# VectorE and ScalarE in written order, and two transposes moved off TensorE, in a hybrid attention and RWKV layer

## The chip, the cores and the metric

The kernel runs on one core of a Trainium2 chip, in one launch. The metric is the device time of one execution in microseconds (us). The core's engines work side by side, each through its own queue in order: TensorE (PE: matmuls, and transposes as matmuls with an identity), VectorE (DVE), ScalarE (ACT), GpSimd (POOL) and SyncE (SP), which here issues nearly all DMAs. Where one engine needs another's result it waits on a semaphore, and all that stands behind it in its queue waits too.

## The reference

One layer over 256 tokens of width 4096, all float32. One projection of the input feeds forgetting attention (FoX: 16 heads of 128), RWKV-7 time mixing (32 heads of 64) and a gate; the gated heads go through an output projection, and a layer norm follows:

```python
proj = einsum('bsd,dc->bsc', x, w_in)      # [fox q|k|v|f, rwkv r|k|v|w|a, gate z]
fox  = softmax(q k^T / sqrt(128) + sum of log f, causal) v
rw   = rw + (rw_prev - rw) * mu_shift      # token shift of the rwkv columns
# per frame: S = S diag(decay) + (S a) b^T + v k^T ;  y = S r
rwkv = groupnorm(y) * gn_gain + gn_bias + bonus
h    = concat(fox, rwkv) * silu(z)
x    = layernorm(ALPHA * x + h @ w_out)
```

The decay and the rate a come from two low-rank ("lora") projections.

## The kernel before

**Main stream.** The weights are read once, in tiles of 128x1024 float32 (two contraction steps of 512 columns). SP loads each by DMA (L220, name w, or wo for the output weights). Each is split into two parts for TensorE's fast float format: ScalarE casts the high half (L141, w_..h) and VectorE subtracts it from the original (L142, w_..l). The input is split the same way, and a product is three matmuls (L147 to L149 in `mm`: high by high, low by high, high by low); a tile is 12 matmuls of 128x512. The input projection runs over 8 pairs n (two groups of 128 channels each) and 4 blocks b of 16 tiles each: b = 0 makes the rwkv r and k, b = 1 the values, b = 2 and 3 the attention's q and k and the gates of one group each. The very first block comes from smaller pieces, together with the lora columns. Then the output projection runs over 8 column blocks of 16 tiles each (`project`, L880 to L882); blocks 0 and 1 are interleaved up to their last tiles, because the last h come late. `weights` keeps three tiles ready: the split of a tile is issued when the matmuls of the tile two before it are.

**Side work.** After every six matmuls `slot()` moves each generator in `sides` on by one `yield`, so a tile has two slots. `wait(W[...])` lets so many slots pass; W holds these numbers. The generators are: `ahead` (`lora`, then `prepare(i)` for each group: decay, its running sum and exponentials, key norms, the matrices BK and lt), `chain` (`forget` for the forget gates, then `rwkv(n)`), `unload` (moves a block's columns from PSUM out, turns them in 32x32 blocks by VectorE, through DRAM and back, and starts `fox(i)`) and `fox` (one attention head).

`rwkv(n)` works on a pair: the 64x64 and 32x32 triangles (gp), a substitution of 31 steps on VectorE (L600 a product, L603 a sum, one step a slot), the values less their mean (L623, SV; ScalarE copies them to UV at L626), further triangles (qt, xp, Q, X), then four chunks in turn (rh, R, up, UV, sp, SV), the readout yp, its norm, and the gated h with its two halves (`gate`, L380 to L384). BK has to be turned for the chunk updates (its turned copy is BKt): in the kernel before by 8 PE transposes a pair (L571) into PSUM and two ScalarE copies of 128x512 (L572). In `fox` the probabilities (lg) are turned the same way, by three PE transposes (L758) and one ScalarE copy of 128x384 (L760) to pT, which the last product (fop, L765) reads.

**Order.** The order of instructions on an engine is set by a scheduler when the program is built. `tc.keep_in_program_order(...)` makes an instruction keep the place in which it was written; `tc.issue_after(...)`, in `behind`, lets some come after the latest split. Before, only SP's DMAs and a few VectorE and ScalarE instructions were held so; the rest was moved by the scheduler.

**Output projection.** `load_tok(b)` loads the residual's columns and the norm's gain and bias, splits the latter (rr, rh, rt, rows: L866 to L872; each one buffer), `add` adds the residual and takes the statistics (L891, L892), `gain` multiplies by the norm's gain (L896) and for the first four blocks splits the result (gh at L899, gl at L900).

Of the kernel before, what the change touches and what calls it, by code (L numbers as in the profile page):

```python
# [17 lines left out]
P = 128  # L18
S = 256
# [26 lines left out]
W = {"fo": 3, "vs": 2, "np": 4, "gp": 5, "tp": 4, "d1": 8, "d2": 12, "xp": 3, "fs": 4, "fp": 5}  # L46
# [38 lines left out]
def layer(ctx: ExitStack, tc: tile.TileContext, xt, xtok, w_main, w_lora, w_first, muv, w_o, up, par, mulora, fbias, lng, lnb, cst, out):  # L85
    nc = tc.nc
    PS = bass.MemoryType.PSUM
# [36 lines left out]
    nc.vector.memset(warm, 0.0)  # L124
    tc.keep_in_program_order(nc.scalar.activation(warm, warm, AF.Tanh))
# [10 lines left out]
    latest = [None]  # L136

    def split(src, n, name, pool=wpool, tag="", cols=1024):
        hi = pool.tile([P, cols], F32R, tag="wh" + tag, name=name + "h", bufs=4 if pool is wpool else 1)
        lo = pool.tile([P, cols], F32R, tag="wl" + tag, name=name + "l")  # L140
        nc.scalar.copy(hi[:, :n], src[:, :n])  # L141
        latest[0] = nc.vector.tensor_tensor(lo[:, :n], src[:, :n], hi[:, :n].bitcast(F32), ALU.subtract)  # L142
        return hi, lo
# [14 lines left out]
    for n, (k0, k1) in enumerate(pieces):  # L158
        for k in range(k0, k1):
            t = xpool.tile([P, 2, S], F32R, tag=f"x{k}", name=f"x{k}")  # L160
            r = x_raw[n][:, (k - k0) * S : (k - k0 + 1) * S]
            tc.keep_in_program_order(nc.scalar.copy(t[:, 0, :], r))
            nc.vector.tensor_tensor(t[:, 1, :], r, t[:, 0, :].bitcast(F32), ALU.subtract)
            xs.append(t)
# [9 lines left out]
    nc.vector.tensor_scalar(half, prm[:, 0:2, :], 0.5, None, ALU.mult)  # L174
    nkk = const.tile([P, G], F32, name="nkk")
    nc.vector.tensor_scalar(nkk, prm[:, PAR.index("k_k"), :], -1.0, None, ALU.mult)
    omm = const.tile([P, 3, G], F32, name="omm")
    nc.vector.tensor_scalar(omm, prm[:, 7:10, :], -1.0, 1.0, ALU.mult, ALU.add)
    oml = const.tile([LORA, 2], F32, name="oml")
    nc.vector.tensor_scalar(oml, mul, -1.0, 1.0, ALU.mult, ALU.add)  # L180
    ika = PAR.index("k_a")
    hka = const.tile([P, 2, G], F32, name="hka")
    nc.vector.tensor_scalar(hka[:, 0, :], prm[:, ika, :], 0.5, None, ALU.mult)
    nc.vector.tensor_scalar(hka[:, 1, :], prm[:, ika, :], -0.5, 1.0, ALU.mult, ALU.add)
    gneps = const.tile([P, 1], F32, name="gneps")
# [37 lines left out]
    def fetch():  # L223
        while len(raws) < 3 and stream:
            load()
        if raws:
# [49 lines left out]
    def lerp(p, mu, om, dst):  # L276
        nc.scalar.mul(dst, p, om)
        nc.vector.scalar_tensor_tensor(dst[:, 1:], p[:, : S - 1], mu, dst[:, 1:], ALU.mult, ALU.add)
# [3 lines left out]
    def issue(out, src):  # L282
        tc.keep_in_program_order(nc.sync.dma_start(out=out, in_=src))
# [19 lines left out]
    for m in range(2):  # L303
        nc.scalar.copy(lw[:, m, :], acc_l[m][:, :LW])
        nc.scalar.copy(bk_0[:, m, :P], acc_l[m][:, LW:LA])
    ff = []

    def lora():
# [9 lines left out]
        nc.vector.tensor_scalar(u, fft[:NF, :S], fb, None, ALU.add)  # L318
        ff.append(u)
        for j in range(2):  # L320
            t = rp.tile([LORA, S], F32, tag="zt", name=f"lw{j}")
            lerp(lt2[:LORA, j * S : (j + 1) * S], mul[:, j : j + 1], oml[:, j : j + 1], t)
            if j == 0:
                nc.scalar.activation(t, t, AF.Tanh)
            nc.scalar.copy(lr[:, j, 0, :], t)
            nc.vector.tensor_tensor(lr[:, j, 1, :], t, lr[:, j, 0, :].bitcast(F32), ALU.subtract)
# [4 lines left out]
    def forget():  # L331
# [5 lines left out]
        nc.vector.tensor_scalar(e, u, -1.0, None, ALU.mult)  # L337
        nc.vector.tensor_tensor(e, e, u, ALU.min)
        nc.scalar.activation(e, e, AF.Exp)
        e1 = ft("fe1")  # L340
        nc.vector.tensor_scalar(e1, e, 1.0, None, ALU.add)
        lg = ft("flg")
        nc.scalar.activation(lg, e1, AF.Ln)
        rest = ft("frest")
        nc.vector.tensor_scalar(rest, e1, -1.0, None, ALU.add)
        nc.vector.tensor_tensor(rest, e, rest, ALU.subtract)
        nc.vector.reciprocal(e1, e1)
        nc.vector.tensor_tensor(rest, rest, e1, ALU.mult)
        nc.vector.tensor_tensor(lg, lg, rest, ALU.add)
        nc.vector.tensor_scalar(u, u, 0.0, None, ALU.min)  # L350
        nc.vector.tensor_tensor(lg, u, lg, ALU.subtract)
        nc.vector.memset(e, 1.0)
        nc.vector.tensor_tensor_scan(rest, e, lg, 0.0, ALU.mult, ALU.add)
        nc.vector.tensor_scalar(lg, rest, -1.0, None, ALU.mult)
# [5 lines left out]
        nc.vector.tensor_copy(ct, ctp[:, : 2 * NF])  # L360
# [8 lines left out]
    def silu2(z, key):  # L369
        th = t256("zt", key + "t")  # L370
        nc.scalar.activation(th, z, AF.Tanh, scale=0.5)
        nc.vector.scalar_tensor_tensor(z, th, 1.0, z, ALU.add, ALU.mult)
        szs[key] = z

    def gate(y, key, k):
# [4 lines left out]
        nc.vector.scalar_tensor_tensor(h, y, 0.5, szs[key], ALU.mult, ALU.mult)  # L380
        pool, tag, bufs = (rp, "hl", 2) if far else (xpool, f"x{k}", 1)
        hl = pool.tile([P, 2, S], F32R, tag=tag, name=f"hl{k}", bufs=bufs)
        nc.scalar.copy(hl[:, 0, :], h)
        nc.vector.tensor_tensor(hl[:, 1, :], h, hl[:, 0, :].bitcast(F32), ALU.subtract)  # L384
# [34 lines left out]
    def front(i):  # L419
        upt = ups[i]  # L420
        uph = rp.tile([LORA, 2, P], F32R, tag="uph", name=f"uph{i}")
        nc.scalar.copy(flat(uph), flat(upt))
        upl = rp.tile([LORA, 2, P], F32R, tag="upl", name=f"upl{i}")
        nc.vector.tensor_tensor(flat(upl), flat(upt), flat(uph).bitcast(F32), ALU.subtract)
# [9 lines left out]
        nc.scalar.activation(tw, lp[:, :S], AF.Tanh, scale=0.5, bias=half[:, 0, i : i + 1])  # L434
        ta = rt(f"ta{i}")
        nc.scalar.activation(ta, lp[:, S:], AF.Tanh, scale=0.5, bias=half[:, 1, i : i + 1])
        yield
        nc.vector.tensor_scalar(tw, tw, -0.5 * DECAY, -0.5 * DECAY, ALU.mult, ALU.add)
        L = rt(f"L{i}")
        nc.vector.tensor_tensor_scan(L, cs[:, C_SCAN : C_SCAN + S], tw, 0.0, ALU.mult, ALU.add)  # L440
        eL = rp.tile([P, NCH, C + 1], F32, tag="eL", name=f"eL{i}")
        nc.gpsimd.memset(eL[:, :, 0:1], 1.0)
        nc.scalar.activation(eL[:, :, 1:], ch(L), AF.Exp)
        eI = t256("eI", f"eI{i}")
        nc.scalar.activation(eI, L, AF.Exp, scale=-1.0)
        yield
        am = t256("am", f"am{i}")
        nc.scalar.activation(am, ta, AF.Identity, scale=hka[:, 0, i : i + 1], bias=hka[:, 1, i : i + 1])
        ae = t256("ae", f"ae{i}")
        nc.vector.scalar_tensor_tensor(ae, ta, 1.0, eI, ALU.add, ALU.mult)  # L450
# [4 lines left out]
    def gather_heads(src, name):  # L455
        t = rp.tile([P, 2 * S], F32, tag="shl", name=f"hq{name}")
        nc.vector.transpose(t, src)
        r = rp.tile([P, 2, QS], F32, tag="hr", name=f"hr{name}", bufs=2)
        nc.vector.tensor_reduce(r[:, 0, :], t.rearrange("p (q f) -> p q f", f=B), AX.X, ALU.add)
# [5 lines left out]
    def spread(dst, val):  # L465
        nc.vector.transpose(dst.rearrange("p (q f) -> p q f", f=B), val.unsqueeze(2).to_broadcast([P, val.shape[1], B]))
# [4 lines left out]
    def prepare(i):  # L471
# [16 lines left out]
        nc.vector.tensor_tensor(k, kr, am, ALU.mult)  # L488
        sb = rp.tile([P, 2, S], F32, tag="Nb", name=f"sb{i}")
        nc.scalar.activation(sb[:, 0, :], kr, AF.Square, scale=column("k_k", i))  # L490
        nc.vector.scalar_tensor_tensor(sb[:, 1, :], r, column("r_k", i), k, ALU.mult, ALU.mult)
# [5 lines left out]
        nc.scalar.copy(q["lc"][:, u, :], eL[:, :, C])  # L497
        nc.vector.scalar_tensor_tensor(lt[0][:, :, 0, :], ch(kr), nkk[:, i : i + 1], eL[:, :, 0:C], ALU.mult, ALU.mult)
        nc.vector.tensor_tensor(lt[0][:, :, 1, :], ch(r), eL[:, :, 1:], ALU.mult)
        nc.scalar.copy(lt[1][HALF[1]], lt[0][HALF[1]])  # L500
        yield
        for j in range(2):
            h = HALF[j]
            nc.vector.tensor_tensor(BK[h, :, KB[j][1]], ch(k)[h], ch(eI)[h], ALU.mult)
        yield from wait(W["np"] if n else 2 * W["np"])
        nc.vector.tensor_tensor(hr[:, 0, :], hr[:, 0, :], hr[:, 1, :], ALU.add)
        n2 = hr[:, 1, : QS // 2]
        nc.vector.tensor_scalar(n2, hr[:, 0, : QS // 2], 1e-24, None, ALU.max)
        nc.vector.reciprocal(n2, n2)
# [5 lines left out]
        nc.vector.scalar_tensor_tensor(ae, ae, 0.5, in2, ALU.mult, ALU.mult)  # L515
        for j in range(2):
            h = HALF[j]
            nc.vector.scalar_tensor_tensor(BK[h, :, KB[j][0]], ch(kr)[h], column("k_k", i)[h], ch(ae)[h], ALU.mult, ALU.mult)
# [3 lines left out]
    def rwkv(n):  # L522
# [27 lines left out]
        for u in range(2):  # L550
            for j in range(2):
                h = HALF[j]
                nc.vector.tensor_tensor(gb[j][h, u], gv[u][j][h], m(h), ALU.mult)
# [3 lines left out]
            nc.sync.dma_start(out=flat(nb[:, u]), in_=nd[u].rearrange("q c r s -> (q c) (r s)").unsqueeze(1).to_broadcast([16, NG, B * B]))  # L557
        for u in range(2):
            for j in range(2):
                o = HALF[1 - j]  # L560
                nc.vector.tensor_tensor(lt[j][o, u], gv[u][j][o].rearrange("p c (x t) -> p c x t", x=2), m(o).rearrange("p c (x t) -> p c x t", x=2), ALU.mult)
# [5 lines left out]
        BKt = rp.tile([P, 2, NCH, P], F32, tag="shl", name=f"BKt{n}")  # L567
        for u in range(2):
            tp = pst(f"tp{n}_{u}")
            for c in range(NCH):  # L570
                nc.tensor.transpose(tp[:, c * P : (c + 1) * P], BK[:, u, c, :], ident)  # L571
            nc.scalar.copy(flat(BKt[:, u]), tp)  # L572
        yield from wait(W["d1"])

        def turns():
            yield from wait(4)
            vst = UVt.rearrange("p u c j v -> p u (c j v)")[:, 0].rearrange("p (m q) -> p m q", m=2)
            for a in range(2):
                tc.keep_in_program_order(nc.vector.transpose(vst[:, a, :], vs_[n][:, a, :]))
# [6 lines left out]
            nc.vector.tensor_tensor(flat(bon), flat(bon), flat(vv[n]), ALU.mult)  # L586
            for u in range(2):
                nc.scalar.activation(bon[:, u], bon[:, u], AF.Identity, bias=column("gn_bias", i0 + u))
# [6 lines left out]
        for u in range(2):  # L595
            nc.scalar.copy(prod[:, u], ev)
            nc.scalar.copy(xc[:, u, :, B - 1 : B], ev[:, :, B - 1 : B])
# [520 lines left out]
```

## Time and profile before

| what | us |
|---|---|
| three runs | 1940.58, 1937.24, 1934.83 (median 1937.24) |
| profiled execution | 1935.4, span 1933.6 |
| tile of the main stream, split to split | 2.72 |
| mean granted TensorE clock | 0.999 of full speed |

In rows of groups, "| 31.0, 704 | 6.6 <-ACT bk" reads: busy 31.0 us in all, 704 ns for one, and 6.6 us of idle time of the engine just before them, most of it ended by that releaser. In the timeline a row is start, duration, engine, line, operation, output and inputs, and in brackets the idle time before it and what ended it. In the list of waits the three numbers are total, times and longest.

### The profile page before, as it was taken

To read this page: it belongs to the slowest core of one execution; us is meant where nothing else is said; L and a number is where in the kernel's file an instruction comes from. 1 tells how busy PE (TensorE), PEld (TensorE's weight loads), DVE (VectorE), ACT (ScalarE), POOL (GpSimd) and SP (SyncE) were. 2 spreads that over 40 slices of the span, in tenths; PEclk is the share of its full clock that TensorE was granted. 3 is DMA by queue.
4 is the path that set the end of the run, shared out by engine and by line. 5 is a ranking of instruction groups with operands and counts; after the bars stand their busy time and mean duration, and the time that the engine had idled before them with its cause. 6 is when DMAs were issued, how large, how long until landed. Compare 5 with 4: busy or idle time off the path is not lost.

```text
span 1933.6 us, 27829 instructions
## 1 busy us (share of the span) xinstructions
PE 1916.5 (99%) x9897; PEld 1594.4 (82%) x9897; DVE 1363.2 (71%) x2323; ACT 963.5 (50%) x1447; POOL 124.2 (6%) x207
## 2 busy tenths in 40 slices
PE   9999999999999999999999999999999999999998
PEld 9888788788888888888888888888888888888886
DVE  6677768857786778677857795779577856755555
ACT  6554464455545644464456444645464554443332
POOL 0020002000200020002000200020001001000000
PEclk9999999999999999999999999999999999999999
DMA  9577667767686778677867677777777777766564
GB/s 343 152 237 229 200 199 215 223 201 216 206 238 198 214 214 236 195 216 211 233 195 220 211 228 202 217 212 220 215 210 221 238 278 242 251 199 197 186 204 166
DMA packets 269391, 420.04 MB, mean 217 GB/s; under 512 B 142338, under 2 KB 169364, under 8 KB 269252
## 3 DMA queue, kind: packets, MB, share of 16 engines
q1 hardware_dynamic: 268820, 417.58, 70.7%
q8 instruction: 77, 1.26, 0.3%
q10 hardware_dynamic: 432, 0.69, 0.1%
q14 instruction: 62, 0.51, 0.1%
HBM read 388.55 MB, written 29.64 MB: 216 GB/s over the span
## 4 chain that ended last, share of the span: by engine, by line
PE 95%; DVE 3%; DMA 1%; issue 0%; ACT 0%; SPq 0%; DVEq 0%; ACTq 0%
PE acc L147 23%; PE acc L149 23%; PE acc L148 23%; PE oacc L880 6%; PE oacc L881 6%; PE oacc L882 6%; PE gp L536 1%; PE rh L647 1%; PE up L678 1%; PE sp L687 1%; PE accl L149 0%; PE accl L148 0%; PE accl L147 0%; PE yp L709 0%; DVE prod L600 0%; DVE xc L603 0%
## 5 line engine op out<-in xcount | busy, mean ns | idle before, releaser
L603 DVE TENSOR_REDUCE xc<-prod 128x8 f32<-128x16 f32 (+30 forms) x248 | 73.1, 295 | 6.5
L600 DVE TENSOR_TENSOR prod<-Nb,xc 128x8 f32<-128x8 f32 (+30 forms) x248 | 71.4, 288 | 6.5 <-DMA Nb<-nd 0.4
L142 DVE TENSOR_TENSOR w_6l<-w,w_6h 128x1024 fp32r<-128x1024 f32 x31 | 37.9, 1222 | 37.5 <-ACT w_6h L141 25.4
L142 DVE TENSOR_TENSOR w_5l<-w,w_5h 128x1024 fp32r<-128x1024 f32 x31 | 41.3, 1333 | 29.5 <-PE acc L149 23.2
L142 DVE TENSOR_TENSOR w_12l<-w,w_12h 128x1024 fp32r<-128x1024 f32 x31 | 38.0, 1227 | 33.5 <-issue 13.8
L740 POOL TENSOR_SCALAR_AFFINE_SELECT nb<-nb 128x128 f32<-128x128 f32 x32 | 15.8, 498 | 705.2 <-DMA nb<-ncd 514.0
L141 ACT CAST w_12h<-w 128x1024 fp32r<-128x1024 f32 x31 | 32.5, 1050 | 48.4 <-DMA w<-in_w_main_dram 19.1
L142 DVE TENSOR_TENSOR w_10l<-w,w_10h 128x1024 fp32r<-128x1024 f32 x31 | 37.9, 1223 | 24.0 <-issue 17.9
L142 DVE TENSOR_TENSOR w_7l<-w,w_7h 128x1024 fp32r<-128x1024 f32 x31 | 37.9, 1222 | 22.1 <-PE acc L149 15.3
L141 ACT CAST w_13h<-w 128x1024 fp32r<-128x1024 f32 x31 | 32.5, 1049 | 40.7 <-PE acc L148 29.0
L141 ACT CAST w_5h<-w 128x1024 fp32r<-128x1024 f32 x31 | 32.6, 1051 | 40.1 <-PE acc L148 37.1
L142 DVE TENSOR_TENSOR w_11l<-w,w_11h 128x1024 fp32r<-128x1024 f32 x31 | 37.9, 1221 | 19.7 <-PE acc L149 19.7
L142 DVE TENSOR_TENSOR w_8l<-w,w_8h 128x1024 fp32r<-128x1024 f32 x31 | 37.8, 1219 | 19.7 <-PE acc L149 15.4
L149 PE MATMUL acc<-w_7l,x 128*128 128x512 f32 x124 | 47.7, 394 | 3.9 <-DVE w_7l L142 3.8
L147 PE MATMUL acc<-w_8h,x 128*128 128x512 f32 x124 | 50.8, 410 | 0.0
L147 PE MATMUL acc<-w_7h,x 128*128 128x512 f32 x124 | 49.9, 403 | 0.2 <-ACT w_7h L141 0.2
L142 DVE TENSOR_TENSOR w_13l<-w,w_13h 128x1024 fp32r<-128x1024 f32 x31 | 37.9, 1222 | 17.2 <-issue 8.3
L147 PE MATMUL acc<-w_3h,x 128*128 128x512 f32 x124 | 49.9, 403 | 0.0
L147 PE MATMUL acc<-w_5h,x 128*128 128x512 f32 x124 | 49.8, 402 | 0.0
L147 PE MATMUL acc<-w_11h,x 128*128 128x512 f32 x124 | 49.8, 402 | 0.0
L147 PE MATMUL acc<-w_15h,x 128*128 128x512 f32 x124 | 49.6, 400 | 0.0
L147 PE MATMUL acc<-w_9h,x 128*128 128x512 f32 x124 | 49.2, 397 | 0.0
(813 smaller groups left out, 6518.7 us busy)
## 6 DMA issues: line engine op xcount, KB each, us to landing
w<-in_w_main_dram SPq DMA_DIRECT2D x496, 512.0 KB, 3.9
wo<-in_w_o_dram SPq DMA_DIRECT2D x128, 512.0 KB, 4.4
bt<-bk SPq DMA_DIRECT2D x88, 128.0 KB, 4.2
Nb<-nd SPq DMA_DIRECT2D x16, 512.0 KB, 4.7
hd<-hl SPq DMA_DIRECT2D x29, 256.0 KB, 3.5
h<-hd SPq DMA_DIRECT2D x29, 256.0 KB, 6.5
wr<-in_w_first_dram SPq DMA_DIRECT2D x15, 384.0 KB, 6.4
lr<-in_w_lora_dram SPq DMA_DIRECT2D x14, 336.0 KB, 5.2
```

The source lines that it names most:

```text
L141: nc.scalar.copy(hi[:, :n], src[:, :n])
L142: latest[0] = nc.vector.tensor_tensor(lo[:, :n], src[:, :n], hi[:, :n].bitcast(F32), ALU.subtract)
L147: nc.tensor.matmul(acc[:, :n], xs[k][:, 0, tt], hi[:, o : o + n], start=(k == 0), stop=False)
L148: nc.tensor.matmul(acc[:, :n], xs[k][:, 1, tt], hi[:, o : o + n], start=False, stop=False)
L149: nc.tensor.matmul(acc[:, :n], xs[k][:, 0, tt], lo[:, o : o + n], start=False, stop=(k == KT - 1))
L536: nc.tensor.matmul(o, BK[h, u, c, :], lt[j][h, u, c], start=True, stop=True)
L600: first = nc.vector.tensor_tensor(prod[:, :, :, s + 1 :], nb[:, :, s : s + 1, s + 1 :].to_broadcast([P, 2, NJ, w]), xc[:, :, :, s + 1 :], ...
L603: nc.vector.tensor_reduce(xc[:, :, :, s : s + 1], prod[:, :, :, s:], AX.X, ALU.add)
L647: nc.tensor.matmul(rh[:, u * P : (u + 1) * P], LT[:, u, c, 0:P], flat(SVt[:, u, c]), start=True, stop=True)
L880: nc.tensor.matmul(acc, ht[k][:, 0, tt], hi, start=(k == 0), stop=False)
L881: nc.tensor.matmul(acc, ht[k][:, 1, tt], hi, start=False, stop=False)
L882: nc.tensor.matmul(acc, ht[k][:, 0, tt], lo, start=False, stop=(k == KT - 1))
```

## The change

`pin` is `tc.keep_in_program_order`, and it is put around nearly every VectorE and ScalarE instruction (splits, casts, side work, output projection); `latest` and `behind` go. Further `yield`s cut side work into smaller lots: in `rwkv` after the DMAs of each u, after the second masks of each u, in the copies of BKt, between the two halves of SV (with the later wait two shorter), after the square root; in `fox` between the exponentials and the reciprocals (the wait fp one shorter); after each `shifted`; between the two `silu2`. W["fo"] goes from 3 to 7. BK's and the probabilities' PE transposes are replaced: VectorE turns 32x32 blocks in place, and copies put the blocks where they belong, 16 of 32 rows a pair for BKt, all by GpSimd and for three of the four chunks, and 16 of 32x96 a head for pT, half by ScalarE and half by GpSimd.

In numbers, over the whole program: TensorE 112 transposes fewer (64 + 48); VectorE 32 transposes more (128x384 each); ScalarE 32 evictions fewer and 128 copies more; GpSimd 256 copies more; SP the same number of DMAs.

```diff
-W = {"fo": 3, "vs": 2, ...
+W = {"fo": 7, "vs": 2, ...
+    pin = tc.keep_in_program_order
...
-        nc.scalar.copy(hi[:, :n], src[:, :n])
-        latest[0] = nc.vector.tensor_tensor(lo[:, :n], src[:, :n], hi[:, :n].bitcast(F32), ALU.subtract)
+        pin(nc.scalar.copy(hi[:, :n], src[:, :n]))
+        pin(nc.vector.tensor_tensor(lo[:, :n], src[:, :n], hi[:, :n].bitcast(F32), ALU.subtract))
...
-        BKt = rp.tile([P, 2, NCH, P], F32, tag="shl", name=f"BKt{n}")
+        BKt = rp.tile([P, 2, NCH - 1, P], F32, tag="shl", name=f"BKt{n}")
         for u in range(2):
-            tp = pst(f"tp{n}_{u}")
-            for c in range(NCH):
-                nc.tensor.transpose(tp[:, c * P : (c + 1) * P], BK[:, u, c, :], ident)
-            nc.scalar.copy(flat(BKt[:, u]), tp)
+            v = flat(BK[:, u, : NCH - 1, :])
+            pin(nc.vector.transpose(v, v))
+        for a in range(4):
+            for b in range(4):
+                nc.gpsimd.tensor_copy(BKt[B * b : B * (b + 1), :, :, B * a : B * (a + 1)], BK[B * a : B * (a + 1), :, : NCH - 1, B * b : B * (b + 1)])
+            if a % 2:
+                yield
...
-            tc.keep_in_program_order(nc.scalar.copy(UV[j][o], SV[j][o]))
+            pin(nc.scalar.copy(UV[j][o], SV[j][o]))
             nc.gpsimd.memset(SV[j][HALF[j], :, 0, :], 0.0)
-        yield from wait(W["d2"] - 1)
+            yield
+        yield from wait(W["d2"] - 3)
...
-        yield from wait(W["fp"])
-        pt = pst(f"fpt{i}")
-        for m in range(3):
-            nc.tensor.transpose(pt[:, m * P : (m + 1) * P], lg[:, m, :], ident)
-        pT = rp.tile([P, 3 * P], F32, tag="nb", name=f"pT{i}")
-        nc.scalar.copy(pT, pt[:, : 3 * P])
+        yield from wait(W["fp"] - 1)
+        pin(nc.vector.transpose(flat(lg), flat(lg)))
+        pT = rp.tile([P, 3, P], F32, tag="nb", name=f"pT{i}")
+        for a in range(4):
+            for b in range(4):
+                pin((nc.gpsimd.tensor_copy if b % 2 else nc.scalar.copy)(pT[B * b : B * (b + 1), :, B * a : B * (a + 1)], lg[B * a : B * (a + 1), :, B * b : B * (b + 1)]))
+        pT = flat(pT)
         yield from wait(W["fo"])
...
-        nc.vector.tensor_scalar(rt_, rh.bitcast(F32), cs[0:6, C_ROW : C_ROW + 1], None, ALU.mult)
-        nc.vector.scalar_tensor_tensor(rows[0:6, o], rr, cs[0:6, C_ROW + 1 : C_ROW + 2], rt_, ALU.mult, ALU.add)
+        pin(nc.vector.tensor_scalar(rt_, rh.bitcast(F32), cs[0:6, C_ROW : C_ROW + 1], None, ALU.mult))
+        pin(nc.vector.scalar_tensor_tensor(rows[0:6, o], rr, cs[0:6, C_ROW + 1 : C_ROW + 2], rt_, ALU.mult, ALU.add))
```

All other hunks put `pin(...)` around an instruction or add one of the yields named above.

More of the change, by code (lines that the diff above doesn't have):

```diff
@@ L1 @@
 import math
-from contextlib import ExitStack, nullcontext
+from contextlib import ExitStack
 import numpy as np
@@ L317, in lora @@
         u = rp.tile([NF, S], F32, tag="t", name="fu", bufs=5)
-        nc.vector.tensor_scalar(u, fft[:NF, :S], fb, None, ALU.add)
+        pin(nc.vector.tensor_scalar(u, fft[:NF, :S], fb, None, ALU.add))
         ff.append(u)
@@ L621, in rwkv @@
                 for a in range(2):
-                    with behind(not n):
-                        nc.vector.scalar_tensor_tensor(
-                            SV[j][o, :, 2 * a + c, :], vm[h, a, :, j].unsqueeze(2).to_broadcast([C, 2, HD]), -1.0 / HD, vt[h, a, :, j, :], ALU.mult, ALU.add
-                        )
-            tc.keep_in_program_order(nc.scalar.copy(UV[j][o], SV[j][o]))
+                    pin(nc.vector.scalar_tensor_tensor(
+                        SV[j][o, :, 2 * a + c, :], vm[h, a, :, j].unsqueeze(2).to_broadcast([C, 2, HD]), -1.0 / HD, vt[h, a, :, j, :], ALU.mult, ALU.add
+                    ))
+            pin(nc.scalar.copy(UV[j][o], SV[j][o]))
             nc.gpsimd.memset(SV[j][HALF[j], :, 0, :], 0.0)
-        yield from wait(W["d2"] - 1)
+            yield
+        yield from wait(W["d2"] - 3)
         for a in range(4):
@@ L641, in rwkv @@
             b = slice(C * j + B, C * j + C)
-            (nc.vector.tensor_copy if j else nc.scalar.copy)(Q[b].rearrange("p u c s -> p (u c s)"), qp[b, : 2 * P])
+            pin((nc.vector.tensor_copy if j else nc.scalar.copy)(Q[b].rearrange("p u c s -> p (u c s)"), qp[b, : 2 * P]))
         def residual(c):
@@ L649, in residual @@
             for j in range(2):
-                (nc.scalar.copy if j else nc.vector.tensor_copy)(R[HALF[j]], diagonal(rh, j))
+                pin((nc.scalar.copy if j else nc.vector.tensor_copy)(R[HALF[j]], diagonal(rh, j)))
             return R
@@ L664, in rwkv @@
             a = slice(C * j, C * j + B)
-            (nc.vector.tensor_copy if j else nc.scalar.copy)(
+            pin((nc.vector.tensor_copy if j else nc.scalar.copy)(
                 X[a].rearrange("p u c t -> p (u c) t")[:, :, C * j + B : C * j + C], xp[a, : 2 * P].rearrange("p (c s) -> p c s", s=B)
-            )
+            ))
         R = residual(0)
@@ L680, in rwkv @@
             for j in range(2):
-                (nc.vector.tensor_copy if j else nc.scalar.copy)(UV[j][HALF[j], :, c, :], uv[HALF[j]])
+                pin((nc.vector.tensor_copy if j else nc.scalar.copy)(UV[j][HALF[j], :, c, :], uv[HALF[j]]))
             yield
@@ L836, in unload @@
                 for t in range(2):
-                    nc.scalar.copy(pair[t], tr[:, t * S : (t + 1) * S])
+                    pin(nc.scalar.copy(pair[t], tr[:, t * S : (t + 1) * S]))
                 yield
@@ L933, in layer @@
                 for m in range(2):
-                    nc.scalar.copy(vt[:, m, :], acc[m][:, 2 * P :])
+                    pin(nc.scalar.copy(vt[:, m, :], acc[m][:, 2 * P :]))
             if b != 1:
@@ L1021, in row @@
         t = rpool.tile([P, P], F32R, name="l" + name)
-        nc.scalar.copy(t, zp[:, :P])
+        pin(nc.scalar.copy(t, zp[:, :P]))
         return t
@@ L1032, in finish @@
         nc.tensor.matmul(wp, l, rows[:, o], start=True, stop=True)
-        nc.vector.scalar_tensor_tensor(res[m][:, o], res[m][:, o], rss[m], wp, ALU.mult, ALU.add)
+        pin(nc.vector.scalar_tensor_tensor(res[m][:, o], res[m][:, o], rss[m], wp, ALU.mult, ALU.add))
     z0, _, last = moments(0)
```

255 lines of the change are left out of this document (129 added, 126 removed).

## Prediction

> **What bounds the kernel now.** I read the page's totals and its chain first, then what TensorE waited for, then one pair of the main loop.
>
> ```profile
> span 1933.6 us, 27829 instructions
> ...
> PE 1916.5 (99%) x9897; PEld 1594.4 (82%) x9897; DVE 1363.2 (71%) x2323; ACT 963.5 (50%) x1447; POOL 124.2 (6%) x207
> ...
> PE 95%; DVE 3%; DMA 1%; issue 0%; ACT 0%; SPq 0%; DVEq 0%; ACTq 0%
> ```
>
> ```profile
> PE acc L149 <- DVE w_7l L142: 3.8, 2, 3.4
> ```
>
> ```profile
> 400.00:591.00 191.00, 191.00 (x1014) 158.59 (x1013) 141.22 (x253) 99.14 (x153) 14.95 (x24) 1.00 0.74 217
> ```
>
> TensorE is the bound: busy 99%, and 95% of the chain. Its worst wait on another engine is 3.8 us in all, for the low half of a weight tile. In the third fence (length, then busy time of PE, weight loads, VectorE, ScalarE, GpSimd; then clock, DMA share, GB/s) one whole pair runs with TensorE never idle and the clock at 1.00, while VectorE works 141 of 191 us. So a pair holds 50 us of free VectorE time, but only if the work lies so that each weight tile is split before TensorE wants it. How much lateness does the kernel bear? VectorE's timeline shows a regular stretch and the one long lot:
>
> ```profile
> 1616.81 1.23 DVE L142 TENSOR_TENSOR wo_5l<-wo,wo_5h 128x1024 fp32r<-128x1024 f32 x1 [1.49 <-PE oacc L882]
> 1619.53 1.22 DVE L142 TENSOR_TENSOR wo_6l<-wo,wo_6h 128x1024 fp32r<-128x1024 f32 x1 [1.49 <-PE oacc L882]
> ```
>
> ```profile
> 368.93 1.21 DVE L142 TENSOR_TENSOR w_6l<-w,w_6h 128x1024 fp32r<-128x1024 f32 x1
> ...
> 371.69 0.38 DVE L600 TENSOR_TENSOR prod<-Nb,xc 128x216 f32<-128x216 f32 x1
> ...
> 376.65 2.00 DVE L623 SCALAR_TENSOR_TENSOR SV<-vm,vs 64x128 f32<-64x128 f32 x8
> 378.68 1.23 DVE L142 TENSOR_TENSOR w_7l<-w,w_7h 128x1024 fp32r<-128x1024 f32 x1
> ```
>
> ```profile
> 379.96 0.50 PE L149 MATMUL acc<-w_7l,x 128*128 128x512 f32 x1 [3.44 <-DVE w_7l L142]
> ```
>
> Undisturbed, a split starts every 2.72 us (one tile), takes 1.23, and leaves 1.49 for side work. Between w_6l and w_7l lay 23 side instructions: the ends of the two splits are 379.91 − 370.14 = 9.77 us apart, 7.05 more than 2.72, and TensorE stood 3.44. So about 3.6 us of lateness is hidden by the tiles in stock and the rest is paid. I call the excess of an interval over 2.72 its slip; slips add up, and a light lot takes back at most 1.49.
>
> **What it removes.** 112 PE transposes leave TensorE, 64 of BK in 8 groups and 48 of the probabilities in 16 groups. One group of each:
>
> ```profile
> 526.40 0.39 PE L149 MATMUL acc<-w_6l,x 128*128 128x512 f32 x1
> 526.63 1.04 PE L571 MATMUL tp<-cs,BK 128*128 128x128 f32 x8
> 527.43 0.48 PE L147 MATMUL acc<-w_7h,x 128*128 128x512 f32 x1
> ```
>
> ```profile
> 391.02 0.39 PE L149 MATMUL acc<-w_10l,x 128*128 128x512 f32 x1
> 391.25 0.49 PE L758 MATMUL fpt<-cs,lg 128*128 128x128 f32 x3
> 391.49 0.48 PE L147 MATMUL acc<-w_11h,x 128*128 128x512 f32 x1
> ```
>
> From weight matmul to weight matmul 527.43 − 526.40 = 1.03 instead of 0.23, so 0.80 a group, times 8 = 6.4. The other: 0.47 − 0.23 = 0.24, times 16 = 3.8. The added yields break up the 23-instruction lot, so its 3.8 us of waits may go too. Together **−14.0**.
>
> **What it adds and moves.** Rows for the costs:
>
> ```profile
> L809 DVE STREAM_TRANSPOSE bk<-bk 128x512 f32<-128x512 f32 x44 | 31.0, 704 | 6.6 <-ACT bk L920 4.2 <-ACT bk L918 2.2
> ...
> L384 DVE TENSOR_TENSOR hl<-h,hl 128x256 fp32r<-128x256 f32 x32 | 13.5, 421 | 8.7 <-ACT hl L383 8.4
> ...
> L891 DVE SCALAR_TENSOR_TENSOR res<-res,oacc 128x512 f32<-128x512 f32 x16 | 10.8, 685 | 9.9 <-PE oacc L882 9.9
> ...
> L579 DVE STREAM_TRANSPOSE UV<-vs 128x256 f32<-128x256 f32 x16 | 6.1, 418 | 0.0
> L872 DVE SCALAR_TENSOR_TENSOR rows<-rr,cs,rt 6x512 fp32r<-6x512 f32 x8 | 5.9, 739 | 0.3
> L871 DVE TENSOR_SCALAR rt<-rh,cs 6x512 f32<-6x512 f32 x8 | 3.8, 474 | 1.6 <-ACT rh L869 0.9
> ```
>
> ```profile
> L141 ACT CAST w_13h<-w 128x1024 fp32r<-128x1024 f32 x31 | 32.5, 1049 | 40.7 <-PE acc L148 29.0
> ```
>
> ```profile
> L693 DVE TENSOR_TENSOR SV<-sp,sl 64x128 f32<-64x128 f32 x32 | 9.2, 289 | 7.3 <-PE sp L687 6.8
> ...
> L750 DVE SCALAR_TENSOR_TENSOR lg<-fsp,ct,nb 128x128 f32<-128x128 f32 x16 | 5.6, 350 | 5.2 <-PE fsp L744 5.0
> ```
>
> ```profile
> L698 ACT ACTIVATE sl<-SV,lc 64x64 f32<-64x64 f32 x64 | 18.7, 338 | 20.4 <-DVE SV L691 11.8 <-DVE SV L693 8.4
> ...
> L626 ACT COPY UV<-SV 64x512 f32<-64x512 f32 x16 | 9.9, 620 | 1.0 <-DVE SV L623 0.4
> ...
> L642 ACT COPY Q<-qt 32x256 f32<-32x256 f32 x8 | 2.9, 363 | 5.9 <-PE qt L638 5.9
> ...
> L497 ACT COPY lc<-eL 128x4 f32<-128x4 f32 x16 | 3.0, 186 | 0.0
> ```
>
> A 128x384 VectorE transpose isn't in the trace: it lies between 0.42 (256 columns) and 0.70 (512); I take 0.55. A 32x96 ScalarE copy lies between 0.19 (4 columns) and 0.36 (256); I take 0.25, nearer the small one. The 16 + 16 transposes are 18 us of VectorE time, the 128 ScalarE copies 32 us against 16 evictions saved: both fit in the free time, so what counts is where they stand in the queue. Pinned, each engine runs in written order, and a weight split or cast that is written behind side work waits for it and for every engine that work waits for. I walked the changed kernel's queues at the thickest places.
>
> *Start (block 0_1), once.* After the split of w_3 the whole lora and forget chain stands in one lot, 22 VectorE instructions, ahead of w_4's split. Before, the same ones lay spread over four tiles:
>
> ```profile
> 72.21 1.23 DVE L142 TENSOR_TENSOR w_3l<-w,w_3h 128x1024 fp32r<-128x1024 f32 x1 [0.46 <-PE acc L149]
> 74.23 0.47 DVE L318 TENSOR_SCALAR fu<-fft,fb 16x256 f32<-16x256 f32 x1 [0.80 <-PE fft L316]
> ...
> 80.32 1.73 DVE L347 RECIPROCAL fe<-fe 16x256 f32<-16x256 f32 x1
> ...
> 86.39 0.15 DVE L360 COPY ct<-ctp 128x32 f32<-128x32 f32 x1
> ```
>
> Their durations, from the first (0.47) to the last (0.15) with the reciprocal's 1.73 and two 0.70 transposes, add up to 10.3. The chain starts at 74.23, so w_4's split ends at 74.23 + 10.3 + 1.23 = 85.8, which is 12.3 after w_3's end at 73.44: slip 9.6, loss 6.0. The next lot (two exponentials on ScalarE between VectorE steps, then the cast) adds some 2, an estimate from hand-overs like these. **+8**; below it 6, above it 10 if ScalarE's hand-overs inside the chain show.
>
> *Output projection, once.* Behind wo1_15's split stand, ahead of wo2_0's: a copy (0.3), rt and rows for column block 0, the same for block 1, four residual steps and two gains (0.68 each), and the low half of the gain block (0.68): 7.5 us. Block 1's row pair shares one buffer, so its DMA waits for rows of block 0, and its cast follows:
>
> ```profile
> 1672.43 0.26 SPq L867 DMA_DIRECT2D rr<-in_lnb_dram  x1
> ```
>
> ```profile
> 1675.44 0.62 ACT L869 CAST rh<-rr 6x512 fp32r<-6x512 f32 x1 [0.74 <-DMA rr<-in_lnb_dram]
> ```
>
> That is 3.0 + 0.6 more, then 0.6 for the cast of the gain block, 0.4 until wo2_0's own cast (1.05) is done, and 1.23: 13.3, slip 10.6, loss 7.0. The lot behind wo2_1 (4.8 + 0.6 + 0.4 + 1.23 = 7.0, slip 4.3, less 1.49 that the tile before gives back) loses 2.8, and two later ones 0.7 each. **+11**, from 4 (if the row DMAs land in good time) to 12.
>
> *Every pair, twice.* First place (last tiles of block 3 to tile 5 of the next): behind the split of tile 12 come two substitution steps (four instructions, 1.2), the bonus product (0.7), the new transpose (0.55); then eight new ScalarE copies (8 × 0.25 = 2.0) ahead of tile 13's cast (1.05) and split (1.23). Interval 6.7, slip 4.0. Three tiles, each with four instructions like the 0.38 row, regain 0.4. The lot with h and its halves goes over to ScalarE and back: 2.7 + 1.23, slip 1.2. Then SV (2.00), its copy (0.62), cast and split: 4.9, slip 2.2. Sum 7.0, less 3.6: 3.4 lost. Second place (tile 14 of block 0 to tile 7 of block 1): two SV sums (0.29 each), four scalings (0.34 each) and a gate product (0.5) ahead of a cast, with cast and split 4.7, slip 2.0; two logits (0.35, the wider some 0.5) with their maxima (0.7 together) and the exponential (0.4) ahead of the next cast, 4.2, slip 1.5; normalising, 0.4; one light tile gives 1.2 back; a pT transpose and eight copies again, 2.4; reciprocal, products and two h chains with casts, 6.0 from end to end, slip 3.3. That comes to 8.4, less 3.6: 4.8. By the full walk 8.2 a pair. (Where an operation has no row here, I took that of its size.) Lower bound nothing: by VectorE's own durations alone (handed-over work hidden) no interval exceeds 6.3 = 2.72 + 3.6. The walk charges every hand-over in full; the row of hl (8.4 us of waits on ScalarE over 32, 0.26 each, not the cast's whole 0.4) says that part hides. I take 5 a pair, times 8: **+40**.
>
> *The copies on GpSimd.* Of these the nearest rows show that they can be held:
>
> ```profile
> 866.97 2.43 POOL L462 COPY hr<-hr 32x16 f32<-32x16 f32 x4 [2.92 <-DVE hr L459]
> ```
>
> ```profile
> 867.33 1.23 DVE L142 TENSOR_TENSOR w_10l<-w,w_10h 128x1024 fp32r<-128x1024 f32 x1
> ```
>
> Four tiny copies took 2.43 us here, across a whole split. At 0.6 each a head's eight take 4.9; fop now stands seven slots of 1.36 behind (9.5), so they are covered, and they cost nothing until each waits for a whole split (9.8). The 16 copies of BKt a pair have longer still.
> The Trainium skill ("SBUF — State Buffer", section "SBUF: two separate sides") calls the port pair that VectorE and GpSimd share an exclusive lock: whichever starts first holds it for its whole instruction, the other blocks. The 2.43 row agrees for GpSimd. By that rule VectorE would also be held by each copy that starts first: with 0.6 for 32 copies a pair at most 19 us, inside the 50 free ones; it would only make the full walk, a rival below, likelier.
>
> **Sum**, against the profiled execution's own 1935.4 us (1.8 more than its span, 1.8 below the runs' median 1937.24): 1935.4 − 14 + 8 + 11 + 40 = **1980**.
>
> **Rivals.**
> *Full walk:* every hand-over shows, 8.2 × 8 = 66, and the upper ends of the one-time terms, 10 + 12: 1935.4 − 14 + 22 + 66 = 2009; what BKt and the forget chain add at other places of a pair, which I didn't walk, can take it past 2020. For it: TensorE has no reserve, and after a stall the next place begins late. Against: 50 us of free VectorE time a pair.
> *Only the two one-time stalls:* steady lots hide wholly. 1935.4 − 14 + 19 = 1940, no change. For it: most steady lots last 1.3 to 2.8 us on VectorE, well below 6.3.
> *The other side, relief prevails:* one mechanism, at every split: order by lots keeps each interval under 6.3 us, the point from which TensorE stands; then the start's lot would have to hide too (its ScalarE parts overlapping, 6 lost) and the output rows arrive early (4 lost): 1935.4 − 14 + 4 = 1925, and down to 1921 with no loss. For it: one lot of 23 cost only 3.4 before. Against: the two one-time lots are longer than that one.
> *It doesn't do what it says:* pinning leaves the order of the steady part nearly as it was, and only the relief and little else shows: 1930.
>
> **How the numbers follow.** The forecast (1955 to 2000) has 0.48, the full walk 0.18, one-time stalls only 0.17, the other side 0.13, no real reordering 0.04. The range 1925 to 2025 leaves out part of the other side and the worst of the full walk. A measurement of this kernel can tell about 0.3% (5.8 us) from no change. Faster: 0.13 + 0.04 = 0.17; same: 0.12 of the one-time case; slower: 0.05 of it + 0.48 + 0.18 = 0.71.
>
> **What would show it.** The groups L571 and L758 gone from TensorE, its chain of waits headed by splits and casts: one wait near 82 us of some 6, several of 1 to 4 at each pair's two places behind pT and UV copies, and 7 then 3 where the output blocks change. If the windows of the pairs stay at 191 us with TensorE full, the third rival holds; if the start shows no wait of over 3 us, my slip rule is wrong; if fop waits for pT, the GpSimd price is.

## The result and the profile after

| kernel | median us | runs | ratio to the kernel before, 95% interval |
|---|---|---|---|
| before | 1937.14 | 1934.83 to 1940.58 | |
| changed | 2033.91 | 2031.5 to 2034.44 | 1.0496 (1.0477 to 1.0514) |

The change costs 97 us, 5.0%. Slower was forecast, at 1980 (43 us); the range ended at 2025, so the size was wrong by more than half. The span grew from 1933.6 to 2032.3. The page's totals and TensorE's list of waits (total, times, longest) of the changed kernel:

```profile
span 2032.3 us, 27997 instructions
...
PE 1955.8 (96%) x9785; PEld 1584.6 (78%) x9785; DVE 1413.4 (70%) x2355; ACT 962.4 (47%) x1543; POOL 218.9 (11%) x463
```

```profile
PE acc L146 <- ACT w_1h L140: 16.7, 14, 1.6
PE acc L146 <- ACT w_5h L140: 12.3, 14, 2.0
PE fop L769 <- POOL pT L764: 5.8, 7, 1.9
PE oacc L887 <- ACT wo_0h L140: 5.7, 1, 5.7
PE yp L708 <- DVE UV L682: 4.1, 7, 0.9
PE ctp L355 <- DVE frest L349: 3.9, 1, 3.9
```

Before, TensorE waited for VectorE's splits, 3.8 us. Now it waits for ScalarE's casts, the high halves: 7 pairs times two places a pair is the "14". Why are the casts late? ScalarE is busy only 47% of the time. The lists of what ScalarE itself waited for answer it, first before, then after:

```profile
ACT prod L596 <- POOL vs L541: 42.3, 8, 5.7
ACT w_5h L141 <- PE acc L148: 37.1, 24, 2.1
ACT w_9h L141 <- PE acc L148: 30.8, 14, 3.7
```

```profile
ACT hl L379 <- DVE h L376: 85.2, 25, 6.9
ACT lt L496 <- DVE lt L495: 77.2, 16, 7.2
ACT R L651 <- DVE R L651: 55.0, 32, 3.6
ACT UV L626 <- DVE SV L623: 52.8, 15, 6.6
ACT lg L754 <- DVE fst L753: 43.6, 32, 4.6
```

Before, ScalarE's waits were mostly casts waiting for TensorE to give a buffer back, that is, ScalarE stood ahead of TensorE. After, it stands at a side copy until VectorE has done its part, up to 7 us at a time, and the next cast stands behind it.

Where the time lies, from the trace: the 7680 weight matmuls, each from its start to the start of TensorE's next instruction, take 1764.8 us before and 1861.7 after (+96.9; 0.227 each where nothing hinders). Of this +9.7 is in block 0_1 (the start), +10.7 in the output projection, and the rest, 76.5, in the pairs, 8 to 14 us each from pair 1 on. The 112 transposes gone save 10.2. Other small products take 12.7 more (qt 3.7, fop 3.2, rh 1.3, yp 1.0). Counted so, a wait falls to the instruction ahead of it: 3.2 us of qt's 3.7 are TensorE's wait for the cast of wo_7, a weight tile. One pair, the same kind of stretch as the 191 us shown before:

```profile
833.00:1036.00 203.00, 196.55 (x1002) 157.65 (x1001) 147.03 (x259) 98.84 (x164) 25.40 (x56) 0.99 0.67 203
```

TensorE idles 6.5 of 203 us, while VectorE has 56 us free and ScalarE 104.

### The profile page after: what moved, and what is told of

Its sections match the earlier page's. It is cut to its first block, busy times and chain, and to the rows that moved or that the text cites. A ratio compares the mean times of both kernels' runs of the same rounds, so it can differ in the third digit from the quotient of the medians.

```text
span 2032.3 us, 27997 instructions
## 1 busy us (share of the span) xinstructions
PE 1955.8 (96%) x9785; PEld 1584.6 (78%) x9785; DVE 1413.4 (70%) x2355; ACT 962.4 (47%) x1543; POOL 218.9 (11%) x463
## 5 line engine op out<-in xcount | busy, mean ns | idle before, releaser
L571 POOL COPY BKt<-BK 32x192 f32<-32x192 f32 x128 | 67.4, 526 | 91.3 <-DVE BK L568 86.3
L146 PE MATMUL acc<-w_1h,x 128*128 128x512 f32 x124 | 50.2, 405 | 16.7 <-ACT w_1h L140 16.7
L146 PE MATMUL acc<-w_5h,x 128*128 128x512 f32 x124 | 52.4, 423 | 12.3 <-ACT w_5h L140 12.3
L141 DVE TENSOR_TENSOR w_3l<-w,w_3h 128x1024 fp32r<-128x1024 f32 x31 | 38.7, 1249 | 23.1 <-ACT w_3h L140 22.9
L148 PE MATMUL acc<-w_5l,x 128*128 128x512 f32 x124 | 50.8, 420 | 3.8 <-DVE w_5l L141 3.7
L141 DVE TENSOR_TENSOR w_0l<-w,w_0h 128x1024 fp32r<-128x1024 f32 x31 | 38.9, 1255 | 20.4 <-ACT w_0h L140 17.1
L146 PE MATMUL acc<-w_13h,x 128*128 128x512 f32 x124 | 50.0, 403 | 1.6 <-ACT w_13h L140 0.7
L146 PE MATMUL acc<-w_0h,x 128*128 128x512 f32 x124 | 49.7, 401 | 1.1 <-ACT w_0h L140 0.9
L146 PE MATMUL acc<-w_14h,x 128*128 128x512 f32 x124 | 49.2, 397 | 1.4 <-ACT w_14h L140 1.4
L146 PE MATMUL acc<-w_2h,x 128*128 128x512 f32 x124 | 50.5, 407 | 0.0
L147 PE MATMUL acc<-w_5h,x 128*128 128x512 f32 x124 | 50.2, 405 | 0.0
```

Of the source, the lines that this page charges most:

```text
L141: pin(nc.vector.tensor_tensor(lo[:, :n], src[:, :n], hi[:, :n].bitcast(F32), ALU.subtract))
L146: nc.tensor.matmul(acc[:, :n], xs[k][:, 0, tt], hi[:, o : o + n], start=(k == 0), stop=False)
L147: nc.tensor.matmul(acc[:, :n], xs[k][:, 1, tt], hi[:, o : o + n], start=False, stop=False)
L148: nc.tensor.matmul(acc[:, :n], xs[k][:, 0, tt], lo[:, o : o + n], start=False, stop=(k == KT - 1))
L571: nc.gpsimd.tensor_copy(BKt[B * b : B * (b + 1), :, :, B * a : B * (a + 1)], BK[B * a : B * (a + 1), :, : NCH - 1, B * b : B * (b + 1)])
```

## The experiments

Two theories. **Order**: the written order holds casts and splits behind side work; the turning itself gives back about the 10 us that TensorE saves. **Copies**: the copies by GpSimd and ScalarE that took the transposes' place cost the time. All runs are beside runs of the kernel before on the same chip (1936 to 1938 us).

### Each half alone

e1 is the changed kernel with the two turns taken back (and fo 3 again):

```diff
-            v = flat(BK[:, u, : NCH - 1, :])
-            pin(nc.vector.transpose(v, v))
+            tp = pst(f"tp{n}_{u}")
+            for c in range(NCH):
+                nc.tensor.transpose(tp[:, c * P : (c + 1) * P], BK[:, u, c, :], ident)
+            pin(nc.scalar.copy(flat(BKt[:, u]), tp))
...
-        pin(nc.vector.transpose(flat(lg), flat(lg)))
...
+            nc.tensor.transpose(pt[:, m * P : (m + 1) * P], lg[:, m, :], ident)
...
+        pin(nc.scalar.copy(pT, pt[:, : 3 * P]))
```

> The order alone: every pin and every added yield of the change, but BK and the probabilities are turned by TensorE and evicted by ScalarE as before (112 PE transposes, 32 evictions), and fo is 3 again. If the written order is what costs, the time stays near the changed kernel's: 2033.9 plus the 10 us of transposes, less the waits for pT and whatever the pT copies delay, so 2025 to 2045. If the copies and transposes that took TensorE's place cost it, most of the 97 us goes: 1945 to 1975.

Measured 2054.28 us, ratio 1.0611 (1.0594 to 1.0629). e2 is the kernel before with the turns put in, unpinned, and fo 7.

> The turning alone: the kernel before, with BK and the probabilities turned by VectorE and moved by GpSimd and ScalarE, fo 7, nothing newly pinned, none of the other yields but the two in the copies of BKt. If order is what costs, the 10 us of transposes on TensorE are won and little is lost: 1922 to 1935, faster than before. If the copies cost it: 1990 to 2025. In between, 1937 to 1960, would mean that GpSimd's copies hold VectorE or delay fop even when the scheduler is free.

Measured 1945.48, ratio 1.0052 (1.0032 to 1.0071). The order alone costs 118 us, more than the whole change: the copies are not the cause. But the turning alone didn't win 10 either; it lost 9. TensorE's waits in e2 show one place:

```profile
PE acc L149 <- DVE w_7l L142: 14.6, 6, 6.8
```

It is the place that cost 3.8 before. In pair 1 substitution and SV stand ahead of w_7's split, now 32 side instructions instead of 23 (13.4 us from the end of w_6's split to that of w_7's, instead of 9.8), and TensorE stood 6.8 us. In pairs 2 to 6 it is 14 substitution instructions instead of 9, without SV (7.0 us instead of 5.0). So the loss is again one of order, this time the scheduler's.

### Which engine's order

In e3, e9 and e7 the changed kernel's `pin` lets one engine go, or the casts alone; the pins of the kernel before stay.

```diff
+    keep = tc.keep_in_program_order
+    def pin(i):
+        return i if "Activation" in str(i.ins.engine) else keep(i)   # e3; e9: "DVE"
...
-        pin(nc.scalar.copy(hi[:, :n], src[:, :n]))                   # e7, with the kept tiles' casts
+        nc.scalar.copy(hi[:, :n], src[:, :n])
```

> The changed kernel with ScalarE's instructions free for the scheduler again (those that were pinned before stay), VectorE pinned. TensorE's waits in the changed kernel are mostly for ScalarE's casts (w_1h 16.7, w_5h 12.3, wo_0h 5.7, wo_7h 3.2 and others, some 43 us). If casts queued behind side copies are the cause: 1980 to 2000. If VectorE's long lots are, with ScalarE's lateness only their echo: 2015 to 2035.

> The counterpart of the run with ScalarE free: ScalarE (casts among it) in written order, VectorE left to the scheduler but for the kernel before's own pins. If what costs is casts that stand behind ScalarE's side work, freeing VectorE helps only where ScalarE waits for a shorter VectorE lot: the time stays within 1985 to 2035. If VectorE's written order is the half that matters, this comes to 1940 to 1960 like the other.

> The changed kernel, everything pinned but ScalarE's casts of the weight tiles, which the scheduler may move ahead of side work. If a cast held behind ScalarE's side work is the cause, this gives most of what freeing all of ScalarE gave (1948.5): 1948 to 1965. If ScalarE's side work among itself (what VectorE waits for) matters as much: 1985 to 2020.

| run | free | median us |
|---|---|---|
| changed kernel | nothing | 2033.91 |
| e9 | VectorE | 2009.74 |
| e7 | ScalarE's weight casts only | 1953.41 |
| e3 | ScalarE | 1948.5 |

Freeing the casts alone takes back 80 of the 97 us; freeing VectorE takes back 24; both runs came where the order theory put them. But e9 is no clean measure of VectorE's written order: of its 24 us 6.4 lie in pair 0, 10.4 behind pair 7 and only 7.4 in pairs 1 to 7, in six of which the scheduler made a new lot of 32 substitution instructions ahead of w_7's split. In e9's list of TensorE's waits:

```profile
PE acc L152 <- DVE w_7l L145: 24.2, 6, 4.0
```

e3 beat its own expectation (1980 to 2000), which came from adding up the waits named after casts: the waits of small products and the slow matmuls behind stalls went with them. In e7 TensorE's list has hardly a cast left, and what remains is at the two ends:

```profile
PE ctp L355 <- DVE frest L349: 6.0, 1, 6.0
PE oacc L889 <- DVE wo_0l L141: 5.6, 1, 5.6
PE oacc L889 <- DVE wo_2l L141: 2.4, 1, 2.4
PE acc L148 <- DVE w_4l L141: 2.3, 1, 2.3
```

### The value shift on GpSimd

The longest stall of most pairs was in block 2, tiles 4 and 5. The changed kernel's timelines of VectorE, GpSimd and ScalarE (start, duration):

```profile
947.92 1.52 DVE L141 TENSOR_TENSOR w_4l<-w,w_4h 128x1024 fp32r<-128x1024 f32 x1
949.36 1.50 DVE L494 SCALAR_TENSOR_TENSOR lt<-s,nkk,eL 128x256 f32<-128x256 f32 x1
950.79 1.51 DVE L495 TENSOR_TENSOR lt<-s,eL 128x256 f32<-128x256 f32 x1
```

```profile
947.07 1.29 POOL L536 TENSOR_TENSOR vs<-vs,bk 128x512 f32<-128x512 f32 x1 [16.19 <-DMA vs<-vd]
948.44 2.14 POOL L537 TENSOR_TENSOR vs<-vs,muv 128x512 f32<-128x512 f32 x1
950.66 1.35 POOL L538 TENSOR_TENSOR vs<-vs,bk 128x512 f32<-128x512 f32 x1
```

```profile
952.33 0.62 ACT L496 COPY lt<-lt 64x512 f32<-64x512 f32 x1 [6.37 <-DVE lt L495]
952.97 1.04 ACT L140 CAST w_5h<-w 128x1024 fp32r<-128x1024 f32 x1
```

While GpSimd runs its two-input steps, each VectorE step with two inputs ends about 1.4 us after the one before, and the cast of w_5 waits 6.37 us behind the copy of lt. e4 leaves two of the three steps out, so the values are not shifted:

```diff
-        nc.gpsimd.tensor_tensor(t, t, muvs[n].unsqueeze(1).to_broadcast([P, 2, 2 * P]), ALU.mult)
-        nc.gpsimd.tensor_tensor(t, t, p, ALU.add)
```

> The changed kernel without two of the three GpSimd steps of the values' token shift (the product with mu and the last sum are left out, so the values are not shifted). In its trace these steps stand beside three VectorE instructions that take 1.5 us instead of 0.42 (lt, twice) and 1.22 (a split), just ahead of the longest stall of each pair (block 2, tiles 4 and 5: 21 us over the pairs above the rest). If GpSimd's two-input steps hold VectorE there, that stall shrinks to under 1 us a pair: 2012 to 2020. If the lot is simply too long: 2028 to 2036.

Measured 2018.86: 15 less, as the first answer said; in pair 4 the stall at these two tiles shrank from 4.0 us to 0.6. VectorE's groups for the second lt step, in before, after, e4 and e3, with the mean in ns behind the busy time:

```profile
L499 DVE TENSOR_TENSOR lt<-s,eL 128x256 f32<-128x256 f32 x16 | 6.5, 409 | 0.0
```

```profile
L495 DVE TENSOR_TENSOR lt<-s,eL 128x256 f32<-128x256 f32 x16 | 13.2, 827 | 0.0
```

```profile
L495 DVE TENSOR_TENSOR lt<-s,eL 128x256 f32<-128x256 f32 x16 | 6.7, 417 | 0.0
```

```profile
L499 DVE TENSOR_TENSOR lt<-s,eL 128x256 f32<-128x256 f32 x16 | 10.0, 624 | 0.0
```

In e3 VectorE is still held (624 ns), yet the pairs lose nothing there: the hold cost time in the changed kernel, where casts stood behind it, and none where they were free. The Trainium skill ("SBUF — State Buffer", section "SBUF: two separate sides") has the lock on the shared ports work both ways; these rows show the side on which VectorE is the one held, by two-input steps of GpSimd.

### The copies of the probabilities

e10 gives all 16 copies a head to GpSimd:

```diff
-                pin((nc.gpsimd.tensor_copy if b % 2 else nc.scalar.copy)(pT[...], lg[...]))
+                pin(nc.gpsimd.tensor_copy(pT[...], lg[...]))
```

> The changed kernel with all 16 copies of the probabilities on GpSimd, so that ScalarE's queue loses the eight that stand ahead of tile 13's cast and, for the other head, of a cast in block 1. My first place puts a slip of 4.0 us of 7.0 on them. If they matter as walked, the stalls behind them go (some 1.5 us at the first place and 1 to 2 at the second, a pair) but fop waits longer for GpSimd (16 x 0.26 instead of 8): 2015 to 2032. If hand-overs elsewhere set the stalls: 2032 to 2045.

Measured 2063.64, a miss. Block 0 of a pair did get 2.0 us shorter (an excess of 1.45 instead of 3.49 in pair 4), as the eight copies ahead of tile 13's cast would have it. That they are the cause isn't shown: TensorE had just stood 6.2 us at fop, time in which the splits could get ahead. And fop cost far more than block 0 gave back:

```profile
PE fop L769 <- POOL pT L764: 45.1, 8, 6.8
```

```profile
L764 POOL COPY pT<-lg 32x96 f32<-32x96 f32 x256 | 105.9, 414 | 663.8 <-DVE lg L760 653.7
```

Sixteen copies now take 16 × 0.41 = 6.6 us, and the VectorE transpose that releases them is itself late. My expectation had priced a copy at 0.26, its mean with eight a head.

### Turning, compared with VectorE pinned

e8 is e3 with TensorE's transposes back (and fo 3 again).

> As the run with ScalarE free and VectorE pinned (1948.5), but BK and the probabilities turned by TensorE as before. The two differ in the turning alone, with no stalls at either in the steady part. If the 112 transposes are worth what their intervals showed (10.2 us) and nothing is paid for the new copies: 1957 to 1961. If GpSimd's and ScalarE's copies eat the gain: 1945 to 1952.

Measured 2002.45, ratio 1.0334 (1.0319 to 1.0348), outside both answers. It stalls at w_15's split in five pairs (16.0 us) and at w_4's in four (12.5). One of the first kind, in VectorE's and ScalarE's timelines of e8:

```profile
800.08 0.42 DVE L384 TENSOR_TENSOR hl<-h,hl 128x256 fp32r<-128x256 f32 x1 [5.01 <-ACT hl L383]
```

```profile
798.70 1.05 ACT L144 CAST w_1h<-w 128x1024 fp32r<-128x1024 f32 x1 [4.36 <-DMA w<-in_w_main_dram]
799.65 0.40 ACT L383 CAST hl<-h 128x256 fp32r<-128x256 f32 x1
```

On ScalarE, free, the scheduler put the cast of h behind the cast of w_1, whose weights hadn't landed; VectorE, pinned, holds w_15's split behind h's low half. One engine in written order and one out of it can cross so, and e8 tells nothing of what the turning is worth. Whether other arrangements of e3 would cross too is open.

### Written order where it helps

e5 frees ScalarE, and VectorE outside pairs 1 to 7; e6 pins nothing new at all. Both have the turns, the yields and the kernel before's own held order.

```diff
+    def pin(i):
+        return keep(i) if steady and "Activation" not in str(i.ins.engine) else i
...
+        if n == 1:
+            steady.append(1)   # e5; not in e6
...
     closed.append(1)
+    steady.clear()
```

> The turning and the yields of the change, with VectorE in written order only from pair 1 to pair 7; ScalarE, and VectorE at the start (pair 0) and in the output projection, are left to the scheduler, with the kernel before's own pins. With ScalarE free the steady part stalled no more than before, and what was left stood at the two ends: a wait of 6 us near 83 and one of 5.6 at the output's block change, some 19 us against the kernel before. If those two lots are the whole rest, 1948.5 - 19 = 1929 (1926 to 1932), faster than the kernel before by what the removed transposes were worth. If the lots cost time only in part, or the scheduler puts other work there: 1936 to 1948.

Measured 1928.38 (1926.89 to 1929.94), ratio 0.9952 (0.9939 to 0.9966): faster than both kernels, and at the forecast. Its page and what is left of TensorE's waits:

```profile
span 1926.6 us, 27997 instructions
...
PE 1910.3 (99%) x9785; PEld 1583.3 (82%) x9785; DVE 1401.4 (73%) x2355; ACT 981.2 (51%) x1543; POOL 238.7 (12%) x463
```

```profile
PE oacc L898 <- ACT wo_7h L146: 1.9, 1, 1.9
PE zp L1041 <- DVE zd L1029: 1.4, 1, 1.4
PE yp L718 <- DVE UV L692: 1.4, 7, 0.2
```

The weight matmuls take 1763.5 us here, 1.4 less than before, the transposes' 10.2 are gone, and the other small products take 2.9 more. So the gain is about what the transposes took. No run has e5's order with TensorE's transposes, so the turning's own share is argued, not shown; and in e2, with the scheduler's order, it won nothing.

> The turning and the yields of the change, nothing newly pinned anywhere (fo 7, fp and d2 as in the change). The turning alone lost most at one lot: 14.6 us of waits for w_7's low half behind SV in six pairs. If the yield between the halves of SV breaks that lot: 1945.5 - 14 = 1931 (1927 to 1935). If the scheduler gathers the lot again whatever the yields: 1940 to 1947.

Measured 1960.48, ratio 1.0121 (1.0107 to 1.0134): a miss. The yields took SV out of the lot, but left free, the scheduler gathered another at the same tile, in six pairs. In TensorE's waits and in VectorE's timeline of e6, where 28 substitution instructions stand between these two splits:

```profile
PE acc L154 <- DVE w_7l L147: 14.9, 6, 2.5
```

```profile
958.68 1.22 DVE L147 TENSOR_TENSOR w_6l<-w,w_6h 128x1024 fp32r<-128x1024 f32 x1
...
968.55 1.21 DVE L147 TENSOR_TENSOR w_7l<-w,w_7h 128x1024 fp32r<-128x1024 f32 x1
```

So VectorE's written order in the steady part gains 32 us here (1928 against 1960), with ScalarE free; it is ScalarE's that costs. With ScalarE in written order VectorE's gains nothing: e9, without it, was 7.4 us shorter in pairs 1 to 7.

## Why the prediction was right or wrong

**The mechanism held.** Splits and casts queued behind handed-over side work, at the start, at the output's first block change and at two places of each pair, as walked.

**The transposes.** 10.2 us was right to the tenth (6.32 + 3.85 in the trace of before), and the 23-instruction lot's stall went too, but not by the yields alone: e6 has them, and a lot still stood at that tile.

**The start** was forecast at 8 and measured 9.7. The wait forecast near 82 of some 6 us came as 3.9 at 83, and the rest as waits near 100 to 110.

**The output projection** was forecast at 11, measured 10.7, and this agreement is partly luck. The lot ahead of wo2_0 ran as walked: from the end of wo1_15's split, 1740.35, to that of wo2_0's, 1754.09, are 13.7 us against 13.3, with the row pair's DMA in it. VectorE's timeline of the changed kernel:

```profile
1740.97 0.74 DVE L879 SCALAR_TENSOR_TENSOR rows<-rr,cs,rt 6x512 fp32r<-6x512 f32 x1
1746.00 0.47 DVE L878 TENSOR_SCALAR rt<-rh,cs 6x512 f32<-6x512 f32 x1 [4.29 <-ACT rh L876]
```

But TensorE stood 5.7 instead of 7.0, so the stock hid 5.3 us and not 3.6, and the later block changes cost nothing. Of the 10.7, 8.7 lie in the 22 us behind 1740: the stall, and 2.9 in slow matmuls after it (last section); 1.6 lie ahead, where pair 7's attention still ran. And there stands a wait that the 10.7 leaves out, because it falls behind a qt product:

```profile
PE oacc L887 <- ACT wo_7h L140: 3.2, 1, 3.2
```

This cast stood behind the exponentials of pair 7's second head, a place that wasn't walked. With it the output projection lost 13.9.

**The pairs** are the step that failed: "I take 5 a pair, times 8: +40". Measured, the pairs cost 76 in weight matmuls and some more in small products. In pair 4 the first place lost 3.4 us (0.6 and 0.4 at tile 5, 1.2 at tile 1, and 1.2 at fop and behind it), the walk's own figure, but partly by luck: SV's copy cost less, and fop, which the walk held to be free, more. The second lost 4.4 against 4.8. A third place, the preparation of the next pair (block 1 tile 13 to block 2 tile 5), which I said I hadn't walked, lost 4.8; over pairs 1 to 7 it was 2.9 to 5.4. So two things failed. I cut the walk from 8.2 to 5, because "part hides" and 50 us of VectorE time were free: free time in a pair is of no use to a cast that is held behind a copy that is waiting, and e7 shows that this alone was 80 us. And the places not walked were put into a rival's upper end instead of the sum. With 8.2 and 3 to 5 a pair the sum would have been 1935.4 − 14 + 19 + 8 × 11.2 = 2030 to, with 8 × 13.2, 2046, against 2033.9.

**GpSimd's copies** weren't free: fop waited for them once in each of seven pairs (5.8 us in all). Their price wasn't the reason. A copy took 0.26, not 0.6, and a head's eight took 2.4 us in pair 4; but VectorE's transpose, which releases them, started only 3.3 us ahead of fop.

**The rivals.** "Full walk" (2009, or past 2020) was the nearest, and the right one in kind. "The other side" fell for the change as made, yet e5, at 1928, comes near that case with the casts free. Its "point from which TensorE stands", 6.3 us, was too low: in pairs 1 to 7 of e5 the ends of two splits are up to 7.06 us apart, and none of TensorE's waits there is for a weight tile. The 3.6 us of hidden lateness behind it had been read from a single lot.

## What to carry to other kernels

When an engine is put into written order, list what each of its instructions waits for, not only how long it runs: a short copy that waits for another engine holds everything behind it, and 53% of free time on that engine doesn't help. Keep the feed of the bounding engine (here the weight casts) out of such a queue, or write it ahead of the side work (the second is not tested here). The scheduler's order is no safe ground either: in e2, e6 and e9 it made lots of its own ahead of w_7's split. When a walk through the queues gives a number, don't discount it by the engine's average idle time, and count the places that weren't walked in the sum.

## What the runs showed of the hardware

A stall can cost more than its length: behind some of them TensorE's granted clock dropped. In the windows of the changed kernel around the stall in block 2 of pair 4 (the seventh figure is the clock):

```profile
952.40:955.40 3.00, 1.15 (x5) 0.37 (x3) 2.00 (x4) 2.98 (x4) 0.98 (x4) 1.00 0.00 0
955.40:959.00 3.60, 3.60 (x10) 2.78 (x11) 3.28 (x7) 1.46 (x2) 0.00 (x0) 0.55 0.69 199
```

```profile
956.40 0.63 PE L148 MATMUL acc<-w_5l,x 128*128 128x512 f32 x1
956.83 0.63 PE L146 MATMUL acc<-w_5h,x 128*128 128x512 f32 x1
```

After 3.0 us with 1.15 busy the mean clock over the next 3.6 us was 0.55, and matmuls started every 0.43 us instead of 0.23. In the changed kernel 48 weight matmuls lasted over 0.6 us, as these do, and in the kernel before none; each loses 0.20, so 9.6 us of the 97 are this. It doesn't follow every stall. The third place of a pair cost 4.8 to 5.4 us in pairs 1, 2 and 4, where the clock dropped, and 2.9 to 3.1 in pairs 3, 5, 6 and 7, where it stayed at 1.00; in pair 5 TensorE had idled 1.2 and 0.5 us there, in pair 4 1.3 and 0.5. What decides it is open. The Trainium skill ("TensorE: Matmul & The Clock Gate", section "Part 1: The HAM clock gate (the "warmup" mystery)") ties the drop to at least one idle window of about 3.4 us; here it came although TensorE had run for more than a third of the 3 us ahead of it.
